# A hybrid attention and mixture-of-experts layer on Trainium2: the experts' slot table built by one-hot products, full-width attention products, 16 KB weight rows and a fifth early expert

## The chip, the cores and the metric

The kernel runs on one core of a Trainium2 chip. A core has TensorE (PE in the profile; PEld is its loading of weights), VectorE (DVE), ScalarE (ACT), GpSimd (POOL) and SyncE (SP), and 16 DMA engines that move data between DRAM, SBUF (the working memory of 128 partitions) and PSUM (where TensorE adds up its products). The metric is the device time of one execution in microseconds. It is compared between kernels as a median over several runs on the same chip.

## The reference

One layer works on 1024 tokens of width 1024. Cut to what matters here:

```python
h = rms_norm(x, ln1_g); proj = h @ w_in
attn = rms_norm(neighbourhood_attention(aq, ak, av, rpb), attn_out_g)   # 8 heads x 64
dn   = bidirectional_gated_deltanet(...)                                # 4 heads x 128, both directions
x = x + concat([attn, dn]) @ w_out
# hierarchical MoE on h = rms_norm(x, ln2_g):
gsel = argmax(h @ wg_r + bg_r)                  # 1 of 8 groups, its softmax probability gp
top_val, top_idx = top_k(expert logits of that group, 2)
gates = gp * softmax(top_val); eid = gsel * 8 + top_idx
# every expert e of 64, for its tokens:
hid = silu(xb @ w_gate[e]) * (xb @ w_up[e]);  y[token] += gate * (hid @ w_down[e])
x = x + y
```

In the attention each of the 16 rows of 64 tokens sees a window of 8 rows by 16 columns. A token goes to exactly two experts, and an expert gets as many tokens as chose it.

## The kernel before

**Up to the attention.** The projections and the DeltaNet scan take the first 545 us and are not touched.

**Attention and out-projection (about 545 to 785 us).** The list `blocks` holds 64 blocks of 128 queries of one head (`half`, head pair `pr`, column window `w`, head `h`). `attn_step(i)` issues the logits of block i, the transposes of block i-2 and the values of block i-3, so that three blocks are in flight. `attn_logits` (L605) makes 384 logits per query in f32r (a rounded format of f32) by two products that add up in `pq`: L617 is the high part of the keys with the high and low parts of the queries stacked over 128 partitions, L618 the low part `kl` of the keys, which has only the 64 rows of one head. VectorE adds the bias and takes the maximum (L621), ScalarE takes the exponential (L623), VectorE divides by the sum (L624, L625). `attn_turn` transposes the result in three squares on TensorE (L631), and ScalarE copies it to `pT` (L633). `attn_values` (L636) multiplies by the values: the two heads of a pair write to the two halves of the 128 output partitions, three products of 64 output partitions and 128 columns each (L641). One f32 product is two passes in the trace. VectorE copies the pair's result to `aT` (L644). Between the blocks the same loop issues the out-projection of the DeltaNet part (`dn_pre`, `dn_turn2`, `dn_mm2`, with `mm3` at L84 to L86: three f32r products of 128x512), and after half of the blocks the list `tail`.

**The tail (about 785 to 838 us).** `tail` runs five stages in a software pipeline over the eight tiles of 128 tokens: `ao_pre`, `ao_mm` (out-projection of the attention part), `router_turn`, `router_pick` (logits, group, two experts, gates: nearly all small VectorE instructions), and `router_rank`. The last finds each token's place among its expert's tokens by products with ones (L863, L864) and a masked sum on VectorE (L866), works out the slot number (L868), and two indirect DMAs per tile from POOL's queue scatter a 16-byte row (token, token, gate, norm factor) to the DRAM table `tbl` at expert * 1024 + rank (L870). The pools decide the final order; the ranks of all tiles and seven of the eight picks fall after 785 us.

**Weights.** `load_w` (L901) loads an expert by three DMAs of 1 MB: gate, up and down, 8 KB per partition and DMA. Four experts are loaded early, each released by a stage of the tail (the end of the attention, `ao_mm` of tiles 4, 6 and 7). There are 7 buffers for gate-and-up pairs and 6 for down (`room`).

**Experts (about 858 to 1437 us).** 32 steps take two experts each, 64 token slots per expert (`CAP`). The table for the slots is read back from DRAM as `tS` by four DMAs (L953, two on ACT's queue and two on SP's): `tS[0]` are ranks 0 to 63, `tS[1]` ranks 64 to 127 for the second pass of those steps that need one. VectorE fills the four gather buffers with zeros (L957). POOL gathers the rows of the tokens from DRAM (L962), TensorE transposes them (L970), multiplies with gate and up (L984) and down (L1002), and POOL adds the result to the output by an indirect DMA (L1005). Gathers run three steps ahead. After step 0's loads, a buffer's next load is issued on SP's queue and waits until the step that used the buffer is done with it.

Of the kernel before, what the change touches and what calls it, by code (L numbers as in the profile page):

```python
# [10 lines left out]
I32 = mybir.dt.int32  # L11
# [25 lines left out]
def tile_layer(ctx, tc, a, out):  # L37
# [545 lines left out]
    for w in range(4):  # L583
        for r in range(4):
            src = av_d.rearrange("(g r c) f -> r c g f", g=4, r=4)[r, KC0[w]:KC0[w] + 32]
            sp.dma_start(vw[r * 32:(r + 1) * 32, w], src)
    blocks = [(half, pr, w, h) for half in range(2) for pr in range(AH // 2) for w in range(4) for h in range(2)]
    qks, lgs, bts, pvs, pTs = {}, {}, {}, {}, {}

    def load_qk(half, pr):  # L590
# [3 lines left out]
        kl = a2.tile([64, 2, 768], F32R, name="kl")  # L594
# [32 lines left out]
    def attn_turn(i):  # L627
        lg = lgs.pop(i)
# [3 lines left out]
        pTs[i] = a2.tile([P, 3, P], F32, name="pT")  # L632
# [33 lines left out]
    atp = mix.enter_context(tc.tile_pool(name="atp", bufs=1, reuse_waits="tile"))  # L666
    aTs.append(atp.tile([P, AH // 2, S // 2], F32, name="aT"))
# [4 lines left out]
    wop = mix.enter_context(tc.tile_pool(name="wop", bufs=1, reuse_waits="tile"))  # L672
# [69 lines left out]
    iot = rc.tile([P, 64], F32, name="iot")  # L742
# [8 lines left out]
    def router_consts():  # L751
# [376 lines left out]
```

## Time and profile before

| | before |
|---|---|
| median of 3 runs | 1443.97 us (1441.38 to 1446.45) |
| profiled execution | 1439.0 us; span of the trace 1437.2 us |
| mean granted clock of TensorE | 0.951 |
| busy in the span: PE, DVE, ACT, POOL | 1254.6 us (87%), 645.8 us, 392.0 us, 374.8 us |
| moved by DMA | 346.97 MB, mean 241 GB/s |

The profiled execution is one run, 5.0 us below the median. Times of the rows below count from the start of its span. A granted clock of 1.00 is 2.4 GHz, 0.50 is 1.2 GHz. A matmul's row gives the time from its start to its modelled end, and matmuls overlap, so the price of one is the distance from its start to the next start. The 16 DMA engines together can show a share slightly above 1.

### The profile page before, as it was taken

How to read it: one execution, taken by the hardware profiler on the slowest of the kernel's cores; microseconds unless marked ns; L12 is line 12 of the kernel's file. 1: busy time of each engine (PE TensorE's matmuls, PEld its weight loads, DVE VectorE, ACT ScalarE, POOL GpSimd, SP SyncE). 2: the span in 40 equal slices, each digit the busy share in tenths (PEclk: the TensorE clock that was granted, in tenths of full speed). 3: DMA queues.
4: the chain of work that ended last, by engine and by line, in shares of the span. 5: the costliest groups of instructions: out<-in, count | busy, mean ns of one | idle time of the engine just before them, and what ended most of it. 6: DMA issues, size and time to landing. Idle time of an engine off the chain costs nothing. (4 is left out here: it accounts for less than half of the span.)

```text
span 1437.2 us, 20602 instructions
## 1 busy us (share of the span) xinstructions
PE 1254.6 (87%) x7425; PEld 840.1 (58%) x7426; DVE 645.8 (45%) x1541; ACT 392.0 (27%) x797; POOL 374.8 (26%) x427
## 2 busy tenths in 40 slices
PE   5988999969989996799999928998988888989985
PEld 4766889969978795477667823443333333423431
DVE  6456853853667643666755841222121121212211
ACT  4445422322354532775444310000000000000000
POOL 2046313021656543122110332112111111111200
PEclk9999999989999997899999959999999999999998
DMA  3261247355565469998673958999999999999981
GB/s 129 72 128 55 67 132 175 96 137 138 167 170 152 121 180 264 255 293 230 181 190 112 352 161 328 385 404 401 394 398 392 389 387 379 375 372 354 378 342 22
DMA packets 128553, 346.97 MB, mean 241 GB/s; under 512 B 53664, under 2 KB 59808, under 8 KB 103600
## 3 DMA queue, kind: packets, MB, share of 16 engines
q1 hardware_dynamic: 88048, 257.60, 50.3%
q0 software_dynamic: 27984, 71.94, 19.1%
q10 hardware_dynamic: 12400, 15.84, 3.2%
q8 instruction: 72, 1.18, 0.3%
q14 instruction: 49, 0.40, 0.1%
HBM read 305.39 MB, written 62.98 MB: 256 GB/s over the span
## 5 line engine op out<-in xcount | busy, mean ns | idle before, releaser
L984 PE MATMUL pp<-wg,xT 128*64 128x512 f32 x1216 | 300.5, 619 | 34.2 <-DMA wg<-in_w_up 25.1
L984 PEld LDWEIGHTS pp<-wg,xT 128*64 128x64 f32 x1216 | 119.5, 142 | 209.5 <-issue 202.2
L1005 POOL DMA_INDIRECT out<-yg,tS x38 | 60.3, 1587 | 409.0 <-DVEq L1050 265.0
L990 DVE SCALAR_TENSOR_TENSOR sg<-pp,tS,sg 128x256 f32<-128x256 f32 x38 | 18.4, 483 | 315.2 <-ACT sg L989 315.2
L1002 PE MATMUL po<-wd,hT 128*64 128x512 f32 x608 | 140.5, 605 | 20.4 <-ACTq L1050 12.6
L84 PE MATMUL pA<-w_hi,h_hi 128*128 128x256 f32 x512 | 151.2, 295 | 0.9 <-issue 0.9
L989 ACT ACTIVATE sg<-pp,tS 128x256 f32<-128x256 f32 x38 | 18.0, 473 | 486.6 <-PE pp L984 486.6
L85 PE MATMUL pA<-w_lo,h_hi 128*128 128x256 f32 x512 | 149.7, 292 | 0.0
L86 PE MATMUL pA<-w_hi,h_lo 128*128 128x256 f32 x512 | 149.7, 292 | 0.0
L1004 DVE TENSOR_SCALAR yg<-po,tS 128x512 f32<-128x512 f32 x76 | 57.1, 751 | 119.9 <-PE po L1002 119.9
L84 PEld LDWEIGHTS pA<-w_hi,h_hi 128*128 128x128 f32 x512 | 100.2, 196 | 2.2 <-issue 1.6
L85 PEld LDWEIGHTS pA<-w_lo,h_hi 128*128 128x128 f32 x512 | 100.2, 196 | 0.2
L86 PEld LDWEIGHTS pA<-w_hi,h_lo 128*128 128x128 f32 x512 | 100.0, 195 | 0.3
L1002 PEld LDWEIGHTS po<-wd,hT 128*64 128x64 f32 x608 | 40.7, 138 | 94.1 <-issue 66.4
L84 PE MATMUL pA<-h_hi,w_hi 128*128 128x512 f32 (+1 forms) x208 | 83.2, 400 | 1.3 <-ACT w_hi L75 1.3
L86 PE MATMUL pA<-h_hi,w_lo 128*128 128x512 f32 (+1 forms) x208 | 82.7, 398 | 0.0
L85 PE MATMUL pA<-h_lo,w_hi 128*128 128x512 f32 (+1 forms) x208 | 82.6, 397 | 0.0
L76 DVE TENSOR_TENSOR w_lo<-w_raw,w_hi 128x512 fp32r<-128x512 f32 (+1 forms) x60 | 40.3, 682 | 85.7 <-ACT w_hi L75 85.4
L970 PEld LDWEIGHTS pt<-ident,xg 128*128 128x128 f32 x304 | 37.4, 195 | 50.7 <-issue 30.0
L641 PE MATMUL pv<-pT,vw 128*64 128x128 f32 x384 | 57.7, 288 | 8.5 <-ACT pT L633 8.4
L239 DVE SCALAR_TENSOR_TENSOR acc<-raw,convw,acc 128x1024 f32<-128x1024 f32 x48 | 63.6, 1334 | 2.5 <-ACT acc L237 2.1
L970 PE MATMUL pt<-ident,xg 128*128 128x128 f32 x304 | 44.9, 291 | 20.5 <-DMA xg<-x_d,tS 20.5
(304 smaller groups left out, 2238.3 us busy)
## 6 DMA issues: line engine op xcount, KB each, us to landing
wd<-in_w_down SPq DMA_DIRECT2D x62, 1024.0 KB, 24.0
wg<-in_w_gate SPq DMA_DIRECT2D x61, 1024.0 KB, 23.7
wg<-in_w_up SPq DMA_DIRECT2D x61, 1024.0 KB, 23.5
bt<-in_bias SPq DMA_DIRECT2D x24, 384.0 KB, 5.4
w_raw<-in_w_nat SPq DMA_DIRECT2D x32, 256.0 KB, 3.6
w_raw<-in_w_dn SPq DMA_DIRECT2D x24, 256.0 KB, 3.1
k<-kk_d POOLq DMA_DIRECT2D x16, 384.0 KB, 8.9
SA_d<-cm POOLq DMA_DIRECT2D x8, 512.0 KB, 2.9
```

Source lines behind the costliest of these rows:

```text
L76: dve.tensor_sub(lo[:, k:k + 2], raw, hi[:, k:k + 2].bitcast(F32))
L84: pe.matmul(dst, sh, mh, start=(i == 0), stop=False)
L85: pe.matmul(dst, sh, ml, start=False, stop=False)
L86: pe.matmul(dst, sl, mh, start=False, stop=(i == n - 1))
L239: dve.scalar_tensor_tensor(acc, raw[:, t:t + S], convw[:, m, t:t + 1], acc, op0=OP.mult, op1=OP.add)
L641: pe.matmul(pv[h * 64:h * 64 + 64], vw[:, w, half + g, hc:hc + AD], pT[:, g], start=(g == 0), stop=(g == 2))
L970: pe.transpose(pt[:, k, :n], xg[:n, g * 4 + k:D:NK], ident[:n, :n])
L984: pe.matmul(pp[d * CAP:(d + 1) * CAP], xT[:, k, d * CAP:(d + 1) * CAP], ws[d][0][:, :, k * 256:(k + 1) * 256], start=(k == 0), stop=(k == ...
L990: dve.scalar_tensor_tensor(sg[:n], pp[:n, 1], mf[:n, 3:4], sg[:n], op0=OP.mult, op1=OP.mult)
L1002: pe.matmul(po[d * CAP:(d + 1) * CAP], hT[:, k, d * CAP:(d + 1) * CAP], w[1][:, k * D + c * 512:k * D + (c + 1) * 512], start=(k == 0), st ...
L1004: dve.tensor_scalar(yg[:n, cs], po[:n], mf[:n, 2:3], None, op0=OP.mult)
L1005: ins = pool.indirect_dma_start(out=out, out_offset=bass.IndirectOffsetOnAxis(ap=meta[:n, 0:1], axis=0), in_=yg[:n], in_offset=None, bound ...
```

## The change

- **Table.** For each tile `router_pick` now also makes `vals`: for each of the token's two choices its one-hot row over 64 experts times three numbers (token minus a large constant, gate, norm factor). `router_rank` makes `ro`, the one-hot row of the rank over 128 ranks, and two f32 products `ro`^T x `vals` (L893) add the tile's entries to the table in `pq`, which VectorE adds to `tab` (128 ranks x 64 experts x 3) in SBUF. After the last tile VectorE cuts `tS` out of `tab` (L972, L973). The scatters to `tbl` stay, since the rare case of an expert with more than 128 tokens reads it.
- **Order.** The gather buffers and `tS` are allocated in the tail, POOL instead of VectorE fills the buffers with zeros, and the last scatters are put behind the first gathers. The memory for this comes from the out-projection's weights and the second `aT`, whose pool is now closed in the tail (`opj`).
- **Fifth expert.** A fifth expert's load is issued right behind the fourth's. The buffers stay 7 and 6.
- **Weight rows.** The host stores gate and up side by side, so a gate-and-up pair is one DMA of 2 MB with 16 KB per partition.
- **Attention.** `kl` gets 64 more partitions that are zero, in two buffers that are cleared once, so that L618 (now L621) is a full 128x128 product. The values of a head pair are one product for both heads (128 output partitions, 256 columns, three per pair, now L646), of which the two diagonal blocks are copied out by two VectorE copies. One of the four `lg` buffers goes.

```diff
+    kls = [a1.tile([P, 2, 768], F32R, name=f"kl{i}") for i in range(2)]
+    for kl in kls:
+        pool.memset(kl[64:128].bitcast(F32), 0.0)
     blocks = [(half, pr, w, h) for half in range(2) for pr in range(AH // 2) for w in range(4) for h in range(2)]
-    qks, lgs, bts, pvs, pTs = {}, {}, {}, {}, {}
...
-        pool.dma_start(kl, heads(kk_d[pr // 2, :, 1, pr % 2, ks]))
+        pool.dma_start(kl[0:64], heads(kk_d[pr // 2, :, 1, pr % 2, ks]))
...
-        pe.matmul(pqv, q2[0:64, h, w * P:(w + 1) * P], kv(kl[:, h]), start=False, stop=True)
+        pe.matmul(pqv, q2[:, h, w * P:(w + 1) * P], kv(kl[:, h]), start=False, stop=True)
-        lg = lgs[i] = a2.tile([P, 384], F32, name="lg", bufs=4)
+        lg = lgs[i] = a2.tile([P, 384], F32, name="lg", bufs=3)
...
...
-        act.activation(pTs[i], pt[:, 0:3], AF.Copy)
+        if h == 0:
+            pTs[i // 2] = a2.tile([P, 3, 2, P], F32, name="pT")
+        act.activation(pTs[i // 2][:, :, h], pt[:, 0:3], AF.Copy)
     def attn_values(i):
         half, pr, w, h = blocks[i]
         if h == 0:
-            pvs[i // 2] = psQ.tile([P, P], F32, name="pv", bufs=1)
-        pv, pT, hc = pvs[i // 2], pTs.pop(i), (pr * 2 + h) * AD
+            return None
+        pv, pT = psQ.tile([P, 2, P], F32, name="pv", bufs=1), pTs.pop(i // 2)
         for g in range(3):
-            pe.matmul(pv[h * 64:h * 64 + 64], vw[:, w, half + g, hc:hc + AD], pT[:, g], start=(g == 0), stop=(g == 2))
-        if h == 1:
-            av = aTs[half][:, pr].rearrange("p (r c) -> p r c", c=64)[:, :, w * 16:w * 16 + 16]
-            return dve.tensor_copy(av, pv.rearrange("p (r c) -> p r c", c=16))
+            pe.matmul(pv, vw[:, w, half + g, pr * P:(pr + 1) * P], pT[:, g], start=(g == 0), stop=(g == 2))
+        av = aTs[half][:, pr].rearrange("p (r c) -> p r c", c=64)[:, :, w * 16:w * 16 + 16]
+        for h in range(2):
+            hs = slice(h * 64, h * 64 + 64)
+            ins = dve.tensor_copy(av[hs], pv[hs, h].rearrange("p (r c) -> p r c", c=16))
+        return ins
...
+        vt = o2.tile([P, 2, 3], F32, name="vt")
+        GATE = vt[:, :, 1]
+        dve.tensor_copy(vt[:, :, 0], tokm[:, t:t + 1].to_broadcast([P, 2]))
+        dve.tensor_copy(vt[:, :, 2], rt[:, 2:3].to_broadcast([P, 2]))
+        vals = o2.tile([P, 2, 64, 3], F32, name="vals", bufs=1)
+        for c in range(2):
+            dve.tensor_tensor(vals[:, c], o64[:, c, :, None].to_broadcast([P, 64, 3]),
+                              vt[:, c, None, :].to_broadcast([P, 64, 3]), op=OP.mult)
+        rts[t] = o64, EID, RNK, row, vals
     def router_rank(t):
-        o64, EID, RNK, row = rts.pop(t)
+        o64, EID, RNK, row, vals = rts.pop(t)
         pn = psQ.tile([P, P], F32, name="pv", bufs=1)
         for u in range(t):
             pe.matmul(pn[:, :64], onesb, oh[:, u], start=(u == 0), stop=False)
         pe.matmul(pn[:, :64], before, oh[:, t], start=(t == 0), stop=True)
         for c in range(2):
             dve.scalar_tensor_tensor(o64[:, c], o64[:, c], 1.0, pn[:, :64], op0=OP.mult, op1=OP.mult, accum_out=RNK[:, c:c + 1])
+        ro = o2.tile([P, 2, P], F32, name="ro", bufs=1)
+        pl = psQ.tile([P, 384], F32, name="pq")
+        for c in range(2):
+            dve.tensor_scalar(ro[:, c], iot, RNK[:, c:c + 1], None, op0=OP.is_equal)
+        for c in range(2):
+            pe.matmul(pl[:, :192], ro[:, c], vals[:, c].rearrange("p e v -> p (e v)"), start=(c == 0), stop=(c == 1))
+        pv3 = pl[:, :192].rearrange("p (e v) -> p e v", v=3)
+        if t == 0:
+            dve.tensor_copy(tab, pv3)
+        else:
+            dve.tensor_tensor(tab, tab, pv3, op=OP.add)
...
-            for j, n in enumerate(("w_down",) if i else ("w_gate", "w_up")):
-                ins = eng.dma_start(w if i else w[:, j], a[n][e].rearrange("(p k) f -> p (k f)", p=P))
-                if after is not None:
-                    tc.add_manual_dep(ins.ins, after.ins.name, mybir.DependencyInfo(how, mybir.DependencyReason.DATA),
-                                      reason="more urgent transfers first")
+            ins = eng.dma_start(w, a[("w_gu", "w_down")[i]][e])
+            if after is not None:
+                tc.add_manual_dep(ins.ins, after.ins.name, mybir.DependencyInfo(how, mybir.DependencyReason.DATA),
+                                  reason="more urgent transfers first")
...
+        if f is ao_mm and t == NT - 1:
+            opj.close()
+            mwB = ctx.enter_context(tc.tile_pool(name="mwB", bufs=1, side="right", reuse_waits="tile"))
+            m1 = ctx.enter_context(tc.tile_pool(name="m1", bufs=1, side="right", reuse_waits="tile"))
+            wt.setdefault(steps[2][1], [[], []])[0] += load_w(mwB, steps[2][1], after=ins)
+            tS = [m1.tile([P, 32, 4], I32, name=f"tS{i}") for i in range(2)]
+            ln2p = m1.tile([P, NK], F32, name="ln2p")
+            act.dma_start(ln2p, a["ln2"][:, 1])
+            LA = 3
+            xgb = [m1.tile([P, D], F32, name=f"xg{i}") for i in range(LA + 1)]
+            for x in xgb:
+                pool.memset(x, 0.0)
+    for tl in range(2):
+        for d in range(2):
+            src = tab[tl * CAP:(tl + 1) * CAP, d * 32:(d + 1) * 32]
+            dst = tS[tl][d * 64:(d + 1) * 64]
+            dve.tensor_scalar(dst[:, :, 0], src[:, :, 0], OOB, None, op0=OP.add)
+            dve.tensor_copy(dst[:, :, 2:4].bitcast(F32), src[:, :, 1:3])
...
-    mwG = ctx.enter_context(tc.tile_pool(name="mwG", bufs=3, reuse_waits="tile"))
-    mwD = ctx.enter_context(tc.tile_pool(name="mwD", bufs=2, reuse_waits="tile"))
+    mwG = ctx.enter_context(tc.tile_pool(name="mwG", bufs=2, reuse_waits="tile"))
+    mwD = ctx.enter_context(tc.tile_pool(name="mwD", bufs=1, reuse_waits="tile"))
     psX = ctx.enter_context(tc.tile_pool(name="psX", bufs=2, space=PSUM, reuse_waits="tile"))
-    ln2p = m1.tile([P, NK], F32, name="ln2p")
-    act.dma_start(ln2p, a["ln2"][:, 1])
-    tS = [m1.tile([P, 32, 4], I32, name=f"tS{i}") for i in range(2)]
-    tv = tbl.rearrange("(d e r) w -> d r e w", d=2, r=S)
-    for tl in range(2):
-        for d in range(2):
-            (act, sp)[d].dma_start(tS[tl][d * 64:(d + 1) * 64], tv[d, tl * CAP:(tl + 1) * CAP])
-    LA = 3
-    xgb = [m1.tile([P, D], F32, name=f"xg{i}") for i in range(LA + 1)]
-    for x in xgb:
-        dve.memset(x, 0.0)
...
+    for i in placed[-2:]:
+        tc.add_manual_dep(i.ins, ins.ins.name, mybir.DependencyInfo(mybir.DependencyClass.NoSync, mybir.DependencyReason.DATA),
+                          reason="the first rows are more urgent")
...
-            mw = mwA if n % room[part] < 4 else (mwG, mwD)[part]
+            mw = mwA if n % room[part] < 4 else mwB if n % room[part] == 4 else (mwG, mwD)[part]
```

The order in which the engines get the work changes at three places. The rows are the program's instructions in their order on one engine; x3 is three alike in a row. The first place is **TensorE in the middle of the attention**: `pt` are the transposes, `pv` the values, `pq` the logits, `pA` the out-projection. Before:

```order
L631 MATMUL pt<-ident,lg 128x128 x3
L641 MATMUL pv<-pT,vw 64x128 x3
L617 MATMUL pq<-k_6231,q_6230 128x384
L618 MATMUL pq<-kl,q_6230 128x384
L631 MATMUL pt<-ident,lg 128x128 x3
L641 MATMUL pv<-pT,vw 64x128 x3
```

After the change:

```order
L634 MATMUL pt<-ident,lg 128x128 x3
L646 MATMUL pv<-pT,vw 128x256 x3
L728 MATMUL pA<-ident,ot 128x128 x4
L620 MATMUL pq<-k_5640,q_5639 128x384
L621 MATMUL pq<-kl_5110,q_5639 128x384
L634 MATMUL pt<-ident,lg 128x128 x3
L620 MATMUL pq<-k_5640,q_5639 128x384
L621 MATMUL pq<-kl_5110,q_5639 128x384
```

The products of 64 output partitions and those of 64 contracted rows are gone; the values come once per pair instead of once per head. The second place is **VectorE at the end of the tail**, from the rank of the last tile on (`cnt` and `ci` are the counts per expert, which decide whether a second pass is run). Before:

```order
L866 SCALAR_TENSOR_TENSOR o_8247,gk<-o_8247,pv 128x64 x2
L868 SCALAR_TENSOR_TENSOR slot<-gk 128x2
L931 COPY cnt<-pv 1x64
L932 TENSOR_TENSOR ci<-cnt 1x32
L934 TENSOR_TENSOR x_8290<-cnt,lim 1x896
L935 TENSOR_REDUCE cnt<-x_8290 1x64
L936 CAST ci<-cnt 1x64
L937 TENSOR_REDUCE lim<-cnt 1x1
L938 CAST ci<-lim 1x1
L957 MEMSET xg_8338 128x1024
```

After the change:

```order
L886 SCALAR_TENSOR_TENSOR o_8255,gk<-o_8255,pv 128x64 x2
L891 TENSOR_SCALAR ro<-iot,gk 128x128 x2
L900 SCALAR_TENSOR_TENSOR slot<-gk 128x2
L898 TENSOR_TENSOR tab<-tab,pq 128x192
L982 COPY cnt<-pv 1x64
L972 TENSOR_SCALAR tS_8052<-tab 64x32
L973 COPY tS_8052<-tab 64x32x2
L972 TENSOR_SCALAR tS_8052<-tab 64x32
L973 COPY tS_8052<-tab 64x32x2
```

The one-hot rows, the addition to `tab` and the first two halves of `tS` now stand between the last rank and the counts' arithmetic, and the fills with zeros are gone from VectorE. The third place is **POOL's queue at the same point**. Before:

```order
L870 DMA tbl<-row,slot 65536x4 x4
L962 DMA xg_8338<-x_d,tS_8332 128x1024
L962 DMA xg_8339<-x_d,tS_8332 128x1024
L962 DMA xg_8340<-x_d,tS_8332 128x1024
L908 DMA wg<-in_w_gate 128x2048
```

After the change:

```order
L966 MEMSET xg_8059 128x1024
L902 DMA tbl<-row,slot 65536x4 x2
L51 TENSOR_TENSOR rt<-rt,mhalf 128x1
L902 DMA tbl<-row,slot 65536x4 x4
L1001 DMA xg_8056<-x_d,tS_8052 128x1024
L1001 DMA xg_8057<-x_d,tS_8052 128x1024
L1001 DMA xg_8058<-x_d,tS_8052 128x1024
L902 DMA tbl<-row,slot 65536x4 x2
```

The fills with zeros now stand ahead of the tail's last scatters, and the gathers ahead of the last tile's two scatters.

## Rows read from the trace of the kernel before

**Rows 1.** The profile's page: costliest groups, and a DMA issue with its median landing.

```profile
L984 PE MATMUL pp<-wg,xT 128*64 128x512 f32 x1216 | 300.5, 619 | 34.2 <-DMA wg<-in_w_up 25.1
...
xg<-x_d,tS POOLq DMA_INDIRECT x38, 11.0
```

**Rows 2.** Busy time by stretch: PE, PEld, DVE, ACT, POOL, clock, DMA share, GB/s.

```profile
594.00:785.00 191.00, 188.65 (x986) 132.60 (x985) 124.46 (x460) 108.61 (x236) 31.09 (x47) 1.00 0.76 206
785.00:824.00 39.00, 39.00 (x250) 33.88 (x248) 31.36 (x142) 14.96 (x33) 13.49 (x16) 1.00 0.95 346
824.00:838.00 14.00, 7.59 (x58) 6.89 (x58) 10.74 (x86) 3.48 (x12) 6.47 (x7) 0.71 1.00 350
838.00:859.00 21.00, 0.58 (x8) 0.40 (x7) 6.78 (x14) 1.28 (x1) 5.82 (x6) 0.50 0.30 30
...
882.00:888.00 6.00, 5.31 (x26) 1.57 (x22) 0.11 (x1) 0.47 (x1) 0.00 (x0) 1.00 0.41 77
888.00:1393.00 505.00, 446.46 (x1998) 188.96 (x2000) 110.08 (x173) 29.52 (x69) 90.28 (x68) 0.98 1.00 384
```

**Rows 3.** TensorE's timeline in the attention: start, duration, line, operation, tile.

```profile
649.07 0.44 PE L617 MATMUL pq<-k,q 128*128 128x384 f32 x1
649.45 0.44 PE L618 MATMUL pq<-kl,q 64*128 64x384 f32 x1
649.82 0.55 PE L631 MATMUL pt<-ident,lg 128*128 128x128 f32 x3
...
655.52 0.40 PE L86 MATMUL pA<-wo_hi,t_lo 128*128 128x512 f32 x1
655.76 0.39 PE L84 MATMUL pA<-wo_hi,t_hi 128*128 128x512 f32 x1
656.08 0.87 PE L641 MATMUL pv<-pT,vw 128*64 128x128 f32 x6
656.88 0.50 PE L85 MATMUL pA<-wo_lo,t_hi 128*128 128x512 f32 x1
657.22 0.39 PE L86 MATMUL pA<-wo_hi,t_lo 128*128 128x512 f32 x1
```

**Rows 4.** TensorE's timeline in the DeltaNet stage: full-width f32 passes of 256 columns.

```profile
441.25 1.13 PE L529 MATMUL ps<-w,kd 128*128 128x256 f32 x4
442.22 1.12 PE L544 MATMUL pw<-wc,at 128*128 128x128 f32 x8
```

**Rows 5.** TensorE's groups, 594 to 785 us: passes, then busy us and mean ns.

```profile
L641 PE MATMUL pv<-pT,vw 128*64 128x128 f32 x352 | 51.5, 283 | 0.1
```

**Rows 6.** VectorE's groups by form, 785 to 838 us.

```profile
L844 DVE TENSOR_SCALAR o<-iot,gk 128x64 f32<-128x64 f32 x14 | 3.0, 256 | 0.1
...
L834 DVE TENSOR_TENSOR ig<-rlg,rt 128x64 f32<-128x64 f32 x7 | 1.9, 271 | 0.1
...
L854 DVE COPY row<-gk 128x2 f32<-128x2 f32 x7 | 1.2, 164 | 0.1
```

**Rows 7.** VectorE's timeline, 836 to 848 us: the slot number behind the last rank.

```profile
838.09 0.16 DVE L868 SCALAR_TENSOR_TENSOR slot<-gk 128x2 int32<-128x2 f32 x1
```

**Rows 8.** POOL's timeline, 835 to 860 us; in brackets the idle time ahead.

```profile
854.73 1.06 POOL L962 DMA_INDIRECT xg<-x_d,tS  x1 [13.73 <-DMA tS<-tbl]
```

**Rows 9.** TensorE's timeline, 830 to 890 us.

```profile
859.15 1.97 PE L970 MATMUL pt<-ident,xg 128*128 128x128 f32 x8 [20.46 <-DMA xg<-x_d,tS]
...
880.22 7.09 PE L984 MATMUL pp<-wg,xT 128*64 128x512 f32 x32 [0.36 <-DVE xT L971]
```

**Rows 10.** SyncE's queue, 820 to 900 us: issues of DMAs.

```profile
823.64 0.33 SPq L908 DMA_DIRECT2D wg<-in_w_gate  x1
...
887.33 0.34 SPq L908 DMA_DIRECT2D wg<-in_w_gate  x1
```

**Rows 11.** DMA queues, 9 to 20 us: packets, MB, share of 16 engines.

```profile
q10 hardware_dynamic: 630, 1.09, 26.2%
q1 hardware_dynamic: 653, 0.51, 14.0%
```

More of the change, by code (lines that the diff above doesn't have):

```diff
@@ L586, in tile_layer @@
             sp.dma_start(vw[r * 32:(r + 1) * 32, w], src)
+    kls = [a1.tile([P, 2, 768], F32R, name=f"kl{i}") for i in range(2)]
+    for kl in kls:
+        pool.memset(kl[64:128].bitcast(F32), 0.0)
     blocks = [(half, pr, w, h) for half in range(2) for pr in range(AH // 2) for w in range(4) for h in range(2)]
-    qks, lgs, bts, pvs, pTs = {}, {}, {}, {}, {}
+    qks, lgs, bts, pTs = {}, {}, {}, {}
     def load_qk(half, pr):
@@ L593, in load_qk @@
         k2 = a2.tile([P, 2, 768], F32R, name="k2")
-        kl = a2.tile([64, 2, 768], F32R, name="kl")
+        kl = kls[pr % 2]
         heads = lambda v: v.rearrange("(h e) t -> e h t", h=2)
@@ L627, in attn_turn @@
     def attn_turn(i):
-        lg = lgs.pop(i)
+        lg, h = lgs.pop(i), blocks[i][3]
         pt = psQ.tile([P, 4, P], F32, name="pt")
@@ L631, in attn_turn @@
             pe.transpose(pt[:, g], lg[:, g * P:(g + 1) * P], ident)
-        pTs[i] = a2.tile([P, 3, P], F32, name="pT")
-        act.activation(pTs[i], pt[:, 0:3], AF.Copy)
+        if h == 0:
+            pTs[i // 2] = a2.tile([P, 3, 2, P], F32, name="pT")
+        act.activation(pTs[i // 2][:, :, h], pt[:, 0:3], AF.Copy)
     def attn_values(i):
@@ L665, in tile_layer @@
     prj.close()
-    atp = mix.enter_context(tc.tile_pool(name="atp", bufs=1, reuse_waits="tile"))
-    aTs.append(atp.tile([P, AH // 2, S // 2], F32, name="aT"))
     rc = mix.enter_context(tc.tile_pool(name="rc", bufs=1, reuse_waits="tile"))
     o2 = mix.enter_context(tc.tile_pool(name="o2", bufs=2, reuse_waits="tile"))
-    wop = mix.enter_context(tc.tile_pool(name="wop", bufs=1, reuse_waits="tile"))
+    opj = ExitStack()
+    atp = opj.enter_context(tc.tile_pool(name="atp", bufs=1, reuse_waits="tile"))
+    aTs.append(atp.tile([P, AH // 2, S // 2], F32, name="aT"))
+    wop = opj.enter_context(tc.tile_pool(name="wop", bufs=1, reuse_waits="tile"))
     dng = rc.tile([P, 1], F32, name="dng")
@@ L741, in tile_layer @@
     br = rc.tile([P, 72], F32, name="br")
-    iot = rc.tile([P, 64], F32, name="iot")
+    iot = rc.tile([P, P], F32, name="iot")
+    tokm = rc.tile([P, NT], F32, name="tokm")
+    tab = rc.tile([P, 64, 3], F32, name="tab")
     tokc = rc.tile([P, NT], F32, name="tokc")
@@ L760, in router_consts @@
         sp.dma_start(br, a["b_r"].to_broadcast([P, 72]))
-        pool.iota(iot, pattern=[[1, 64]], base=0, channel_multiplier=0, allow_small_or_imprecise_dtypes=True)
+        pool.iota(iot, pattern=[[1, P]], base=0, channel_multiplier=0, allow_small_or_imprecise_dtypes=True)
         pool.iota(tokc, pattern=[[P, NT]], base=0, channel_multiplier=1, allow_small_or_imprecise_dtypes=True)
+        dve.tensor_scalar(tokm, tokc, -OOB, None, op0=OP.add)
         pool.memset(onesb, 1.0)
@@ L838, in router_pick @@
         dve.tensor_copy(mf[:, 1], mi[:, 1])
-        gk = o2.tile([P, 3, 2], F32, name="gk")
-        GATE, EID, RNK = (gk[:, i] for i in range(3))
+        gk = o2.tile([P, 2, 2], F32, name="gk")
+        EID, RNK = (gk[:, i] for i in range(2))
+        vt = o2.tile([P, 2, 3], F32, name="vt")
+        GATE = vt[:, :, 1]
         dve.scalar_tensor_tensor(EID, gs.to_broadcast([P, 2]), 8.0, mf[:, 1, 0:2], op0=OP.mult, op1=OP.add)
@@ L843, in router_pick @@
         for c in range(2):
-            dve.tensor_scalar(o64[:, c], iot, EID[:, c:c + 1], None, op0=OP.is_equal)
+            dve.tensor_scalar(o64[:, c], iot[:, 0:64], EID[:, c:c + 1], None, op0=OP.is_equal)
         dve.tensor_tensor(oh[:, t], o64[:, 0], o64[:, 1], op=OP.add)
@@ L1019, in tile_layer @@
     loads = [(2 * j + d, part) for j in range(2, NS) for part in range(2) for d in range(2)]
+    loads = [l for l in loads if l[0] != 4]
     first = next(i for i, (n, part) in enumerate(loads) if n == room[part])
@@ L1092, in layout @@
     a["b_r"] = np.concatenate([g["router_group_b"][0], g["router_expert_b"][0]])[None]
-    a["w_gate"], a["w_up"], a["w_down"] = (g[f"expert_w_{n}"][0] for n in ("gate", "up", "down"))
+    gate, up, down = (g[f"expert_w_{n}"][0].reshape(64, P, 2048) for n in ("gate", "up", "down"))
+    a["w_gu"], a["w_down"] = np.stack([gate, up], 2), down
     a["w_out"] = g["w_out"][0].reshape(NK, P, D).transpose(1, 0, 2)
```

2 lines of the change are left out of this document (removed).

## The prediction, made before the changed kernel was run

> **What bounds the kernel now.** I went from the end to the start. In the expert stage one product, L984, has 300.5 us of TensorE's time and most of its waits there are for the weights' DMAs [rows 1]. From 888 to 1393 us the DMA engines have a share of 1.00 at 384 GB/s while TensorE is busy 446 of 505 us [rows 2]: the stage is bound by the weights that are still to come (64 pairs of gate and up less the 7 that fit, 64 downs less 6: 180 MB), and it moves as a whole when its start moves. The start is bad: from 838 to 859 us TensorE works 0.58 of 21 us and the DMAs carry 30 GB/s [rows 2]. This gap is the way through the table in DRAM. Ahead of it, 594 to 785 us, TensorE is busy 188.65 of 191 us with VectorE at 124 and ScalarE at 109: what comes off TensorE there comes off the time until VectorE or ScalarE is full. In the tail, 785 to 824, TensorE is busy all 39 us, but VectorE 31.36 of them, and from 824 to 838 VectorE has 10.74 of 14 us and TensorE 7.59. So TensorE bounds the first half of the change, VectorE is second in the tail, a chain of single steps bounds the table, and DMA the rest.
>
> **Attention.** The two logit products of a block start 0.38 us apart and the next operation 0.37 later: 0.75 us a block. An out-projection product of 512 columns and full width starts 0.24 after its like (655.52 to 655.76) [rows 3], so 384 columns are worth 0.18 and the pair 0.36. Between a saving of nothing (384 columns cost what they cost) and 0.39 I take 0.30, near the upper end, since the out-projection's passes are of the same f32r kind. The values of one head take 0.80 (656.08 to 656.88); the interval ahead of them is 0.32 and the one behind 0.34 where alike neighbours have 0.24, so 0.18 more, and a pair costs 1.96. Six full-width f32 passes of 256 columns cost 0.24 each (four in 0.97 us) [rows 4], 1.45 in all. That is 0.5 per pair; where a value product stands next to L618 the two share such a step, so I take 0.4. The stretch has 352 passes [rows 5], six per block: 58 blocks or 29 pairs, and 55 blocks of logits, as these run three ahead. 55 x 0.30 + 29 x 0.4 = 28 us less for TensorE; the bounds are 4 (0.15 a pair, nothing for logits) and 36.
>
> The longer intervals stand only beside products that use 64 columns or 64 rows. The Trainium skill, "TensorEngine Tiling (Array Packing)", section Key Properties, says that a change of the tiling mode drains TensorE. The trace agrees, with 0.08 to 0.10 us beside L641; if narrow products had no such price, the values would give only 4 of the 12 us and the sum would be 8 us higher.
>
> VectorE has one more copy per pair, 29 x 0.27 (a 128x64 form) [rows 6] = 8 us. It then has 132 of 163 us, 82%, ScalarE 67%. With three blocks in flight, one step late shows, so I count four fifths of 28: **-22** (bounds 0 and -30). The first load of `kl` comes behind two clears; that is under 2 us of POOL's time ahead of the stretch and inside the bounds.
>
> **Tail.** VectorE's additions per tile, by their nearest rows: two small copies at 0.16; two products to `vals`, 128x192, between 0.27 (one of 64 columns) and three times that, taken at 0.37, since most of a 64-column instruction is a fixed part (128x2 costs 0.16); two `ro` at 0.26; one addition to `tab` at 0.37 [rows 6]. That is 1.06 in a pick and 0.89 in a rank. Seven picks and eight ranks lie between 785 and 838: 14.5 us on 42.1 of 53. It does not fit (56.6): at least 3.6 us are exposed, at most 14.5. Since VectorE's instructions there wait for each other and for TensorE, I take 10, half of it before 824: **+5**, the other half in the next part. The four fills by POOL cost VectorE nothing, as POOL has 13.5 of 39 us.
>
> **Table.** Before: the instruction behind the last rank's masked sums starts at 838.09 [rows 7]. POOL issues the first gather at 854.73, after 13.73 us of waiting for `tS` [rows 8], and TensorE transposes at 859.15 [rows 9]: 21.1 us, of which the gather itself is 4.4. After: two `ro` 0.52; four passes of 192 columns, 0.18 each at full clock and 0.36 at the granted 0.50 of this stretch, 1.3; `tab` 0.37; the counts' copy 0.2; the four instructions of `tS[0]` 0.8; the gather 4.4; handovers between engines 0.4. That is 8.0, so 13 us less, with 5 of the tail against it: **-8**. The fifth expert lies across it: the fourth's load is issued at 823.64 [rows 10] and keeps the DMAs busy to 838; 3.1 MB more at 384 GB/s end near 846. If the tail is 5 us longer, the gather is issued there and finds the queues free; if it isn't, the gather lands like those of the expert stage, 11.0 instead of 4.4 [rows 1]. Either way about 851. I keep -3 to -13. Scatters behind the gathers wait for nobody.
>
> **Fifth expert by itself: 0.** Between 882 and 888 the DMAs carry 77 GB/s [rows 2] although most weights are still to come: all 7 and 6 buffers are full. SP's next load is issued at 887.33 [rows 10], when the second pass of step 0 is done with its gate-and-up product (880.22 + 7.09) [rows 9]. The number of buffers is the same after, so loading the fifth sooner only fills them sooner. What moves the bound stage is that step 0 starts, and so frees buffers, 8 us earlier. That is in the sum.
>
> **16 KB rows.** Two queues in a quiet stretch of 11 us (176 us of engine time) spend 26.2% on 630 packets and 1.09 MB and 14.0% on 653 packets and 0.51 MB [rows 11]. Both fit 8.5 ns per packet and 37.4 us per MB, an estimate from these two rows. Half the packets of the 57 gate-and-up pairs behind the gap saved, 57 x 128 x 8.5 ns / 16 = 3.9 us: **-4** (0, if the hardware cuts them up again, to -5). TensorE's 34.2 us of waits for weights [rows 1] can take that up.
>
> **Sum:** -22 + 5 - 8 - 4 = -29 on the profiled execution's 1439.0 us (its span is 1437.2): 1410. The median of the runs shown is 5.0 above that execution, so the forecast is **1415 us**.
>
> **Rivals.** (a) *The attention gives little* (0.17): the 0.37 us are what 384 columns cost, or VectorE's 82% in a chain PE, VectorE, ScalarE, VectorE, PE holds TensorE up. For it: ScalarE and VectorE have waits of their own in each block. Against: TensorE waited for nearly nothing in 191 us. With -4 there, -11 in all: 1433. (b) *All of it comes* (0.12): -30, tail 0, -10, -4 make -44: 1400. (c) *The fifth expert gives its 8 us as well* (0.08), if the buffers fill later than I think: 1407. Against it stands the idle DMA at 882. (d) *Slower* (0.08): VectorE becomes the bound of attention and tail. All 14.5 us of the tail and the 8 us of copies are exposed and TensorE's saving turns into waits: +22.5 - 13 - 4 = +5.5, 1449. It decides from the point where VectorE's work of a block exceeds TensorE's; by the rows it has 132 against 163 us, so it would need 30 us more than I count. That the change does not do what it says shows in (a).
>
> **How the numbers follow.** The forecast has 0.55. The range 1399 to 1435 takes in (a), (c) and about half of (b), and leaves out (d) and the rest; the likeliest case alone has 1406 to 1424. Within 0.3% (4.3 us, about what a measurement of this kernel can tell from no change) are part of (a) and part of (d), 0.07; slower is most of (d), 0.05; faster the rest, 0.88.
>
> **What would show it.** Right: value products of 256 columns starting about 0.24 us apart; the logit pair in 0.36 to 0.45; no added interval beside them; the stretch from 594 to 785 some 22 us shorter with TensorE still near 100%. In the tail VectorE above 90% and `ao_mm` of tile 7 about 17 us earlier rather than 22. First transposes about 8 us after the last masked sum. The DMAs idle again before the first buffer comes free, as at 882. A GB/s one per cent higher from then on. Wrong: TensorE with waits for `lg` or `pT` in the attention; a gather that takes 10 us; or a first free buffer that does not come earlier though step 0 starts earlier.

## The result, and the profile after

The changed kernel takes 1426.86 us (median of 4 runs, 1423.81 to 1431.12) against 1442.85 us for the kernel before on the same chip: ratio 0.9888, 95% interval 0.9855 to 0.992. That is 16 us less (12 to 21), where 29 were forecast. The profiled span is 1424.4 us against 1437.2; the profiled execution of the kernel before (1439.0 us) lies 4 us below this median and that of the changed kernel (1426.66) at its median, so differences between the two traces run 3 to 4 us short of the 16. Where the two traces stand at the same points of the program (us from the start of the span; "later" is after minus before):

| point of the program | before | after | later |
|---|---|---|---|
| VectorE takes the logits of block 8 | 593.61 | 586.15 | -7.5 |
| the same of block 63, the last | 778.16 | 774.39 | -3.8 |
| last out-projection of the attention part ends on VectorE | 823.61 | 823.25 | -0.4 |
| last masked sum of the ranks ends | 838.05 | 840.22 | +2.2 |
| first transposes of gathered rows | 859.15 | 848.44 | -10.7 |
| first load behind a freed buffer | 887.33 | 875.61 | -11.7 |
| end of the span | 1437.2 | 1424.4 | -12.8 |

So the table gave what it was to give, and of the attention, the largest term of the sum, hardly anything is left at the last out-projection. The stretches of the changed kernel, with the columns of [rows 2] (PE, PEld, DVE, ACT, POOL, clock, DMA share, GB/s):

```profile
586.20:823.30 237.10, 207.14 (x1065) 168.35 (x1065) 174.07 (x669) 123.34 (x268) 48.55 (x67) 0.95 0.80 230
823.00:840.00 17.00, 11.32 (x69) 10.29 (x70) 13.73 (x106) 3.81 (x12) 6.69 (x8) 0.65 0.95 342
840.00:848.00 8.00, 2.25 (x12) 1.52 (x11) 4.91 (x23) 1.28 (x1) 3.09 (x4) 0.50 0.65 249
868.00:875.00 7.00, 6.59 (x33) 2.21 (x32) 1.04 (x2) 0.00 (x0) 1.66 (x1) 1.00 0.32 49
876.00:1382.00 506.00, 444.51 (x2002) 167.02 (x2004) 110.16 (x173) 29.70 (x70) 90.31 (x68) 0.98 0.98 385
```

The first row is the stretch from block 8's logits to the last out-projection; below it is called **the stretch**. TensorE is idle for 30 of its 237 us. Before it had next to no idle time there [rows 2], as the same stretch of that kernel shows:

```profile
593.60:823.60 230.00, 227.65 (x1234) 166.68 (x1233) 155.82 (x603) 123.96 (x269) 44.59 (x63) 1.00 0.79 230
```

TensorE does get its saving, 20.5 us of busy time, and the stretch is not shorter for it. In these two traces it is 7 us longer, 3.7 of them up to block 63 and 3.4 in the tail. Two experiments below leave the code of the stretch as it is in the changed kernel (e7) and in the kernel before (e8); their rows:

```profile
591.30:825.00 233.70, 204.27 (x1065) 166.39 (x1065) 174.23 (x669) 123.40 (x268) 48.56 (x67) 0.96 0.82 234
598.00:831.90 233.90, 232.26 (x1233) 170.04 (x1233) 155.99 (x603) 124.13 (x269) 44.82 (x63) 0.97 0.77 226
```

So single traces of the same code differ by 3 to 4 us here. That the stretch is no shorter is shown, that it is longer is not. What TensorE waits for in the changed kernel's stretch, longest first (total, times, longest):

```profile
PE pq L620 <- DVE mx L624: 9.9, 6, 4.2
PE pA L84 <- ACT t_hi L731: 5.7, 1, 5.7
PE pA L84 <- ACT wo_hi L693: 3.8, 2, 2.6
PE pt L634 <- DVE mx L627: 3.5, 2, 2.2
PE pt L634 <- DVE lg L628: 3.4, 3, 1.9
```

These are waits for VectorE and ScalarE, and these two wait for loads: 39 us together in the changed kernel's stretch, where it is 9 in that of the kernel before. The two longest of the changed kernel, then the longest of the kernel before:

```profile
ACT wo_hi L693 <- DMA wo_raw<-in_w_out: 16.6, 5, 5.9
DVE lg L624 <- DMA bt<-in_bias: 9.5, 4, 3.0
```

```profile
ACT wo_hi L685 <- DMA wo_raw<-in_w_out: 6.4, 3, 4.3
```

One wait of TensorE over all engines, 634.9 to 639 us:

```profile
636.22 0.76 DVE L770 TENSOR_TENSOR wr<-wr,ln 128x576 f32<-128x576 f32 x1 [4.33 <-DMA wr<-in_w_r]
637.57 0.55 DVE L624 CUSTOM_DVE_ANT_0 lg<-pq,bt 128x384 f32<-128x384 f32 x1
...
638.18 0.69 PE L620 MATMUL pq<-k,q 128*128 128x384 f32 x1 [4.22 <-DVE mx L624]
```

VectorE's instructions stand here in the program's order. One of them (L770, which scales the router's weights) stands for 4.33 us behind a load; the maximum of a block (L624) is queued behind it; TensorE stands for 4.22 us because that maximum must free `pq`. The products themselves came out as read. TensorE's timeline:

```profile
639.68 0.79 PE L84 MATMUL pA<-wo_hi,t_hi 128*128 128x512 f32 x1 [0.49 <-DVE ms L719]
640.27 0.63 PE L85 MATMUL pA<-wo_lo,t_hi 128*128 128x512 f32 x1
...
648.76 0.39 PE L86 MATMUL pA<-wo_hi,t_lo 128*128 128x512 f32 x1
648.99 0.34 PE L620 MATMUL pq<-k,q 128*128 128x384 f32 x1
649.17 0.34 PE L621 MATMUL pq<-kl,q 128*128 128x384 f32 x1
649.35 0.49 PE L634 MATMUL pt<-ident,lg 128*128 128x128 f32 x3
...
650.42 1.56 PE L646 MATMUL pv<-pT,vw 128*128 128x256 f32 x6
651.82 0.60 PE L728 MATMUL pA<-ident,ot 128*128 128x128 f32 x4
...
848.44 1.97 PE L1009 MATMUL pt<-ident,xg 128*128 128x128 f32 x8 [5.91 <-DMA xg<-x_d,tS]
```

The logit pair takes 0.36 us (648.99 to 649.35) where it took 0.75 [rows 3], the six passes of a value pair 1.40 (650.42 to 651.82) where two heads took 1.96, and no longer interval stands beside them.

### The profile page after: what moved, and what is told of

The parts are those of the page before. It is cut to its first block, busy times and chain, and to the rows that moved or that the text cites. A ratio compares the mean times of both kernels' runs of the same rounds, so it can differ in the third digit from the quotient of the medians.

```text
span 1424.4 us, 20268 instructions
## 1 busy us (share of the span) xinstructions
PE 1230.5 (86%) x7265; PEld 820.3 (58%) x7266; DVE 663.0 (47%) x1634; ACT 391.3 (27%) x797; POOL 379.2 (27%) x428
## 5 line engine op out<-in xcount | busy, mean ns | idle before, releaser
L1023 PE MATMUL pp<-wg,xT 128*64 128x512 f32 x1216 | 296.8, 613 | 37.3 <-DMA wg<-in_w_gu 24.1
L1023 PEld LDWEIGHTS pp<-wg,xT 128*64 128x64 f32 x1216 | 96.1, 141 | 232.2 <-issue 189.8
L84 PE MATMUL pA<-w_hi,h_hi 128*128 128x256 f32 x512 | 150.5, 294 | 0.7 <-issue 0.7
L85 PE MATMUL pA<-w_lo,h_hi 128*128 128x256 f32 x512 | 149.1, 291 | 0.0
L86 PE MATMUL pA<-w_hi,h_lo 128*128 128x256 f32 x512 | 149.0, 291 | 0.0
L84 PEld LDWEIGHTS pA<-w_hi,h_hi 128*128 128x128 f32 x512 | 99.7, 195 | 1.6 <-issue 1.1
L85 PEld LDWEIGHTS pA<-w_lo,h_hi 128*128 128x128 f32 x512 | 99.8, 195 | 0.2
L86 PEld LDWEIGHTS pA<-w_hi,h_lo 128*128 128x128 f32 x512 | 99.4, 194 | 0.3
L84 PE MATMUL pA<-h_hi,w_hi 128*128 128x512 f32 (+1 forms) x208 | 83.6, 402 | 1.8 <-ACT w_hi L75 1.8
L85 PE MATMUL pA<-h_lo,w_hi 128*128 128x512 f32 (+1 forms) x208 | 83.2, 400 | 0.0
L86 PE MATMUL pA<-h_hi,w_lo 128*128 128x512 f32 (+1 forms) x208 | 82.8, 399 | 0.0
L84 PE MATMUL pA<-wo_hi,t_hi 128*128 128x512 f32 x128 | 54.4, 425 | 10.0 <-ACT t_hi L731 5.7
L75 ACT ACTIVATE w_hi<-w_raw 128x512 fp32r<-128x512 f32 (+1 forms) x60 | 35.5, 611 | 76.2 <-DMA w_raw<-in_w_nat 37.6
## 6 DMA issues: line engine op xcount, KB each, us to landing
k<-kk_d POOLq DMA_DIRECT2D x16, 384.0 KB, 10.7
```

Source lines behind the costliest of these rows:

```text
L75: act.activation(hi[:, k:k + 2], raw, AF.Copy)
L84: pe.matmul(dst, sh, mh, start=(i == 0), stop=False)
L85: pe.matmul(dst, sh, ml, start=False, stop=False)
L86: pe.matmul(dst, sl, mh, start=False, stop=(i == n - 1))
L1023: pe.matmul(pp[d * CAP:(d + 1) * CAP], xT[:, k, d * CAP:(d + 1) * CAP], ws[d][0][:, :, k * 256:(k + 1) * 256], start=(k == 0), stop=(k == ...
```

## The experiments

The theories, as the expectations name them. **A**: TensorE's saving is real, but VectorE and ScalarE stand behind loads, and TensorE had covered that. **B**: three `lg` buffers instead of four hold TensorE. **C**: the added VectorE copies and VectorE's own work do.

**e1: the attention part alone, on the kernel before.** All attention lines of the diff ahead of the prediction, among them:

```diff
-        pe.matmul(pqv, q2[0:64, h, w * P:(w + 1) * P], kv(kl[:, h]), start=False, stop=True)
+        pe.matmul(pqv, q2[:, h, w * P:(w + 1) * P], kv(kl[:, h]), start=False, stop=True)
-        lg = lgs[i] = a2.tile([P, 384], F32, name="lg", bufs=4)
+        lg = lgs[i] = a2.tile([P, 384], F32, name="lg", bufs=3)
```

> The kernel before with the attention part alone (full-width logits and values, three lg buffers). Theory A (the saving on TensorE is real, but VectorE and ScalarE stand still behind loads, and TensorE had covered that): TensorE's busy time falls by 22 to 26 us, its waits between 545 and 785 us rise by about as much, and the time falls by 0 to 6 us, 1437 to 1443. The recorded forecast: 22 us less, 1421.

Measured: 1431.15 us (10 runs) against 1442.35, ratio 0.993, interval 0.9911 to 0.995: 10 us less. Neither number was hit: the forecast gave 22 less, theory A at most 6. From 545 to 785 us TensorE is busy for 20.5 us less (196.53 instead of 217.08), where theory A had 22 to 26, and idle for as much longer. In the trace the last out-projection ends at 817.71, 5.9 us sooner, all of it gained ahead of block 8 (587.27 instead of 593.61); the stretch is as long as before, with TensorE idle for 27.6 us of it:

```profile
587.30:817.70 230.40, 202.83 (x1047) 164.82 (x1048) 166.69 (x633) 123.61 (x268) 44.98 (x63) 0.96 0.82 233
```

The other 4 us of the shorter span lie behind the last out-projection, where executions differ by as much anyway (see e4). Why the first eight blocks went faster was not tested.

**e2: the changed kernel without the attention part.**

```diff
-        kl = kls[pr % 2]
+        kl = a2.tile([64, 2, 768], F32R, name="kl")
...
-            pe.matmul(pv, vw[:, w, half + g, pr * P:(pr + 1) * P], pT[:, g], start=(g == 0), stop=(g == 2))
+            pe.matmul(pv[h * 64:h * 64 + 64], vw[:, w, half + g, hc:hc + AD], pT[:, g], start=(g == 0), stop=(g == 2))
```

> The changed kernel with the attention part undone. If attention is worth 4 us at most (theories A, B and C alike): 1427 to 1432, and the last out-projection of the attention ends within 4 us of the changed kernel's. If it was worth what was forecast and the longer tail ate it: 1445 or more.

Measured: 1434.39 us, ratio 0.9952, interval 0.9929 to 0.9975: the table, the fifth expert and the rows together give 7 us. With e1's 10 that is 17, and the whole change measured 16: the two halves add up within their intervals. The expectation was 2 us too low. Its second half was missed by more: the last out-projection was to end within 4 us of the changed kernel's, and it ends at 834.89, 11.6 us later. Without any of the attention part the stretch is longer than before (230.0), in e1 (230.4) and in the changed kernel (237.1):

```profile
595.10:834.90 239.80, 235.48 (x1246) 172.69 (x1244) 162.75 (x638) 122.70 (x267) 48.76 (x67) 0.97 0.76 223
```

The longer tail is 3.7 us of it; most of the rest is TensorE's busy time at the lower clock. So inside the changed kernel the attention part is worth more at this point than on the kernel before (6 us in e1), by single traces.

**e3: four `lg` buffers in the changed kernel.**

```diff
-        ev = npool.tile([P, 2, 256], F32, name="ev")
+        ev = npool.tile([P, 2, 256], F32, name="ev", bufs=1)
...
-        lg = lgs[i] = a2.tile([P, 384], F32, name="lg", bufs=3)
+        lg = lgs[i] = a2.tile([P, 384], F32, name="lg", bufs=4)
```

> The changed kernel with four lg buffers instead of three (room made by one buffer less for the projections' results). Theory B (the third buffer holds TensorE): 10 us less or more, about 1416, and TensorE's waits for lg and for the maxima are halved. Theory A: within 3 us of the changed kernel, 1424 to 1430.

Measured: 1436.61 us, ratio 0.9961 to the kernel before, 10 us slower than the changed kernel. The run isn't clean, since `ev` lost a buffer for it: block 8's logits come at 597.37, 11 us late, 6 of which are there at block 0 (570.45 instead of 564.40), where `lg` can't matter yet. From there to the last out-projection it takes 238.5 us where the changed kernel takes 237.1. So theory B finds no support, though the run can't bound a smaller effect.

**e4: one bias tile.**

```diff
-            bts[half, pr, w] = a2.tile([P, 2, 384], F32, name="bt")
-            sp.dma_start(bts[half, pr, w], a["bias"][pr, w - w // 2, half])
+            if i == 0:
+                bts[0] = a2.tile([P, 2, 384], F32, name="bt", bufs=1)
+                sp.dma_start(bts[0], a["bias"][pr, w - w // 2, half])
+            bts[half, pr, w] = bts[0]
```

> The changed kernel with one bias tile loaded once and used for all blocks: the other 23 loads of 384 KB are left out, so that all but the first blocks get a wrong bias. Theory A: TensorE's waits between 560 and 785 us, some 35, fall below 18, and the time falls by 10 us or more, to 1416 or less. Theory B and theory C (the added VectorE copies): at most 4 us less, 1423 or more.

Measured: 1413.63 us, ratio 0.9794, interval 0.9751 to 0.9837. The time met theory A, the mechanism did not: the stretch is only 3 us shorter, as long as in e7 with all its bias loads, and TensorE is idle for 27 us of it.

```profile
584.40:818.30 233.90, 207.09 (x1079) 169.85 (x1078) 175.62 (x676) 124.24 (x270) 49.86 (x69) 0.95 0.72 201
```

Up to the last out-projection 5 us are won; 6 more appear after the first freed buffer (542.4 us to the end instead of 548.8), in a stage that the edit reaches only through the wrong routing (39 passes instead of 38). This part differs by some us between profiled executions anyway (549.9 before, 547.2 in e1, 545.8 in e2), so a total alone tells little here, and the next runs were read by the stretch.

**e5 and e6: neither bias nor output weights loaded, in the changed kernel (e5) and in the kernel before (e6).** e4's edit and:

```diff
-                raw = wop.tile([P, 512], F32, name="wo_raw", bufs=2)
-                sp.dma_start(raw, a["w_out"][:, half * 4 + k, n:n + 512])
+                if "wo" not in bts:
+                    bts["wo"] = wop.tile([P, 512], F32, name="wo_raw")
+                    sp.dma_start(bts["wo"], a["w_out"][:, half * 4 + k, n:n + 512])
+                raw = bts["wo"]
```

> The changed kernel with one bias tile and one raw tile of the out-projection's weights, each loaded once and used throughout: 23 bias loads of 384 KB and 15 weight loads of 256 KB are left out, so that bias and output weights are wrong; every engine's work stays. Theory A (loads hold VectorE and ScalarE, and these TensorE): from the logits of block 8 to the end of the last attention out-projection, 237 us in the changed kernel and 234 with one bias tile, 220 or less; time 1403 or less. Theory C (VectorE's own work and the chain between the engines): 230 or more, time 1408 or more.

> The kernel before with the same loads left out. Theory A says that TensorE covered them there: the same stretch, 230 us in the kernel before, stays at 224 to 230, and what is saved is at the attention's start only: time 1425 to 1440. If loads bound this kernel as well, the stretch falls by as much as in the changed kernel, to 215 or less.

The false weights change the routing, so that the expert stage has more passes (1945 and 1983 us in all); only the stretch counts. First e5, then e6:

```profile
586.60:796.50 209.90, 201.89 (x1083) 167.45 (x1081) 173.84 (x675) 123.80 (x269) 49.48 (x68) 0.99 0.72 198
```

```profile
583.20:816.50 233.30, 231.67 (x1243) 170.48 (x1244) 158.04 (x611) 125.76 (x273) 46.30 (x64) 0.98 0.63 174
```

This decides it. Without these loads the changed kernel's stretch falls by 27 us (24 from e7's), to 209.9 with 8 us of idle time on TensorE. The kernel before gains nothing from the same edit (233.3, where it has 230.0 and 233.9 with the loads): TensorE is busy for all but 1.6 us of it. With the loads the change doesn't shorten the stretch, without them it shortens it by 23, although the tail in it got longer. From block 8 to block 63 alone 161.1 us are left of 187.9: 27 of the 28 us that the prediction had for TensorE. The VectorE work is the same in e5 and in the changed kernel (174 us), so theory C falls. And e5 has three `lg` buffers, so theory B can hold no more than some of the 8 us that are left.

**e12: only the output weights not loaded**, in the changed kernel (e5 without e4's edit).

> The changed kernel with one raw tile of the output weights, loaded once (15 loads of 256 KB left out, so that the output weights are wrong and with them the routing: only the time up to the router counts); the bias is loaded as ever. If the conversion of the weights is what holds VectorE and ScalarE: from block 8's logits to the last attention out-projection 218 us or less, most of the 27 us that leaving out both brought. If it is the sum of the loads: 224 to 232, and TensorE's waits go on behind the bias and the DeltaNet outputs.

```profile
586.70:807.50 220.80, 205.93 (x1083) 170.71 (x1081) 174.09 (x675) 123.85 (x269) 49.58 (x68) 0.97 0.82 229
```

This is one execution. The stretch is 16 us shorter, between the two expectations (218 or less, 224 to 232). The bias alone was worth 3, no more than traces of the same code differ by, and both together 27: the weights hold most, and the rest shows once they are gone.

**e9 and e10: six raw buffers instead of two**, in the changed kernel (e9) and in the kernel before (e10).

```diff
     prj.close()
+    rwp = e4.enter_context(tc.tile_pool(name="rwp", bufs=6, side="right", reuse_waits="tile"))
...
-                raw = wop.tile([P, 512], F32, name="wo_raw", bufs=2)
+                raw = rwp.tile([P, 512], F32, name="wo_raw")
```

> The changed kernel with six instead of two buffers for the raw output weights (in a pool that lives only as long as the attention). Theory A, in its form after the runs with loads left out (the conversion of the output weights, two loads at a time, holds VectorE and ScalarE): from block 8's logits to the last attention out-projection 228 us or less instead of 237, ScalarE's waits for raw weights (16.6 us) below 8, time 1420 or less. The rival (what is short is the DMA engines' bandwidth in that stretch, not the number of buffers): at most 3 us less, 1423 or more, and the waits move to other loads.

> The kernel before with six buffers for the raw output weights. Theory A: TensorE is busy throughout and covers the conversion, so the same stretch stays within 3 us of 230 us and the time within 5 us of the kernel before, 1438 to 1445. If the buffers cost time there too: 8 us less or more, 1435 or less.

Measured: e9 1428.3 us, ratio 0.9897 (0.9868 to 0.9926), no gain on the changed kernel; e10 1455.75 us, ratio 1.0081 (1.0051 to 1.0111), 12 us slower than before, which neither theory had expected. e9 in two stretches, 560 to 600 us and the stretch:

```profile
560.00:600.00 40.00, 18.78 (x77) 13.77 (x76) 22.00 (x77) 21.97 (x42) 9.17 (x16) 0.65 0.92 235
600.00:828.60 228.60, 209.15 (x1077) 170.80 (x1075) 172.60 (x666) 119.45 (x262) 48.40 (x67) 0.96 0.81 229
```

The stretch does fall to 228.6, by 8.5 us (5 from e7's), and ScalarE's waits for raw weights from 16.6 to 6.5 us. The time is the rival's and the waits are theory A's, so these runs don't tell whether buffers or bandwidth is short. But block 8 comes at 600.04, 14 us later: the first eight blocks take 30.0 us instead of 21.7. In e10 they take 34.3 instead of 27.9, and its stretch is longer too, 241.1, where theory A had 227 to 233. The attention begins while the DMA engines are already full (share 1.03 from 560 to 600 in the changed kernel), and more weights loaded ahead there delay what the blocks need first. That the start got longer is measured; that the order of these loads is the reason is argued, and why e10's stretch got longer is open.

**e11: six raw buffers, and the table in DRAM cleared during the DeltaNet stage.** e9's edit and:

```diff
...
+    pad = dnp.tile([P, 32, 4], I32, name="pad")
+    pool.memset(pad[:, :, 1:4], 0.0)
+    pool.memset(pad[:, :, 0:1], int(OOB))
+    for b in range(64 * S // (32 * P)):
+        sp.dma_start(tblv[b], pad)
     dec.close()
...
-        for b in range(64 * S // (32 * P)):
-            sp.dma_start(tblv[b], pad)
```

> The changed kernel with six raw buffers, and the 16 transfers that clear the table in DRAM (1 MB in rows of 512 bytes) issued during the DeltaNet stage instead of in the middle of the attention. If the burst of loads around 600 to 630 us holds VectorE: 3 to 6 us less than with six buffers alone. If not: within 3 us of it.

Measured: 1428.35 us, ratio 0.9904 (0.9874 to 0.9933), the same as e9. Moving the clearing transfers out of the attention brings nothing that could be measured. Its stretch:

```profile
598.90:833.20 234.30, 210.50 (x1076) 171.91 (x1075) 172.20 (x666) 119.11 (x262) 48.27 (x67) 0.95 0.77 218
```

With the same six buffers this is as long as e7's with two, so the shorter stretch of e9 is not confirmed.

**e7: the fifth expert not early.**

```diff
-            wt.setdefault(steps[2][1], [[], []])[0] += load_w(mwB, steps[2][1], after=ins)
...
-    loads = [l for l in loads if l[0] != 4]
```

> The changed kernel with the fifth expert's load no longer behind the fourth's, but with the other loads of step 0, behind the first gathers. The recorded forecast (the buffers are full before the first comes free either way): 1424 to 1430, the first load behind a freed buffer at most 2 us later, and the DMAs still idle before it. The rival (the early load is worth its 3.1 MB): 6 to 8 us more, 1432 to 1436.

Measured: 1424.98 us, ratio 0.9882 (0.9843 to 0.9922), the same as the changed kernel's 0.9888. The first load behind a freed buffer comes at 876.35 instead of 875.61. One detail was wrong: the DMAs are not idle ahead of it, they are still at the load that came later. SyncE's first issue there and the stretch ahead of it:

```profile
876.35 0.34 SPq L939 DMA_DIRECT2D wg<-in_w_gu  x1
```

```profile
868.00:876.00 8.00, 7.58 (x40) 2.84 (x38) 1.78 (x3) 0.00 (x0) 1.65 (x1) 1.00 1.00 395
```

In the changed kernel the same place has a share of 0.32 (868 to 875, above). The early load moves work into a gap and leaves another gap behind.

**e8: 16 KB rows alone, on the kernel before.**

```diff
-            for j, n in enumerate(("w_down",) if i else ("w_gate", "w_up")):
-                ins = eng.dma_start(w if i else w[:, j], a[n][e].rearrange("(p k) f -> p (k f)", p=P))
...
+            ins = eng.dma_start(w, a[("w_gu", "w_down")[i]][e])
...
```

> The kernel before with gate and up side by side, one load of 16 KB rows per pair. The recorded forecast: 4 us less (0 to 5), 1437 to 1443, and half the packets of the weights' queue for gate and up. If the hardware cuts rows at 8 KB: the same packets and the same time.

Measured: 1440.18 us against 1443.27, ratio 0.9973, interval 0.9944 to 1.0003: the forecast's 4 us, but not told apart from nothing. The packets do fall, from 128,553 to 119,336; 64 x 128 = 8,192 of that are the halved gate-and-up rows; the page's row of e8:

```profile
DMA packets 119336, 346.96 MB, mean 240 GB/s; under 512 B 52640, under 2 KB 58784, under 8 KB 102576
```

No run was faster than the changed kernel beyond its interval and still computed the whole layer.

## Why the prediction was right in direction and too large

**The step that failed** is in the part on the attention: "With three blocks in flight, one step late shows, so I count four fifths of 28". TensorE's saving was read rightly. Its price rows came true (0.36 for the pair, 1.40 for the values), and without the loads its busy time in the stretch falls from 231.67 to 201.89 us, 30 against the 28 of the sum. But of the 22 that were counted next to none is seen in the stretch (e1: 230.4, against 230.0 us before and 233.9 in e8). The 10 us by which e1 is faster lie elsewhere: 6 ahead of block 8, for which the sum has no term, and the rest behind the stretch. That the total came as near to the forecast as it did is in part luck. I took VectorE's 82% and ScalarE's 67% as room. An average of busy time says nothing of an engine that stands in order behind a load. In the kernel before, the two stood 9 us behind loads in the stretch and TensorE was idle for 2; with a faster TensorE they stand for 39 and TensorE is idle for 30. The DMA share of 0.76 in [rows 2] was in front of me and I did not ask what the loads would do to a faster TensorE. The sign of being wrong that the prediction names, TensorE with waits for `lg` or `pT`, came true (3.4 and 1.6 us). Rival (a) (4 us there, 1433 in all) came nearer than the forecast, and had half the cause: VectorE does hold TensorE up, but behind loads, not by its own work.

**The clock took a part.** The changed kernel's stretch has a granted clock of 0.95 where the kernel before has 1.00 and e5 0.99, and the same products take 207.14 us busy in it and 201.89 in e5. So some 5 us of the loss are the clock. The two longest of the three pieces at 0.50:

```profile
586.20:599.40 13.20, 6.90 (x16) 5.18 (x17) 8.01 (x27) 8.60 (x14) 1.02 (x1) 0.50 1.09 302
637.00:643.80 6.80, 5.13 (x14) 3.83 (x14) 5.23 (x21) 2.86 (x7) 1.61 (x2) 0.50 0.60 230
```

The first came over from the attention's start. The second begins in the 4.22 us wait shown above, and the third (725.7 to 729.1) just behind a wait of 2.6 us. In the second L84 and L85 start 0.59 us apart where like products took 0.24 [rows 3]. A lower mean does not need long waits in the stretch: e8 has 0.97 with 1.7 us of idle time in it.

**The joins.** With one width throughout, L86 to L620 is 0.23 us again (648.76 to 648.99), without the 0.08 to 0.10 that stood beside the narrow products. The Trainium skill, "TensorEngine Tiling (Array Packing)", Key Properties, says that a change of the tiling mode drains TensorE; the trace agrees.

**Tail: +5 and +5 forecast, +6 measured.** From block 63's logits to the last out-projection 48.9 us instead of 45.5, and from there to the last masked sum 17.0 instead of 14.4. VectorE is at 13.73 of 17 us (second row of the stretches), 81%, where the prediction's sign was above 90%. The prices were right: `vals` 0.35 (0.37 forecast), `ro` 0.28 (0.26), `tab` 0.35 (0.37).

**Table: 8.0 us forecast, 8.2 measured** (840.22 to 848.44). The one-hot products took 1.65 us at a clock of 0.50, 0.35 more than counted; 0.14 of that is a slip in the sum, since four times 0.36 is 1.44 and not 1.3. POOL's first gather was issued at 843.99, and its rows were there 4.4 us later:

```profile
843.99 1.06 POOL L1001 DMA_INDIRECT xg<-x_d,tS  x1 [5.53 <-issue]
```

With the tail's 2.5 us against it this part gives -10 where -8 was forecast. The step 0 that starts 10.7 us sooner frees its first buffer 11.7 us sooner (875.61), and the bound stage moves as a whole, as the prediction said.

**Fifth expert: 0 forecast, 0 measured** (e7). Rival (c) falls. **Rows: -4 forecast, -3 (8 less to nothing) measured** (e8). In the changed kernel the GB/s of the bound stage, which were to be one per cent higher, are 385 where they were 384 [rows 2].

Rival (d), slower, would have needed VectorE as the bound; it has 174 of 237 us. The terms as measured, -10 for the attention, -12.9 + 6 for table and tail, 0 and -3, make -20; the measured -16 has an interval of -12 to -21.

What stays open: why the first eight blocks went faster, and whether an order of the loads exists that gives the whole 22. In e9 the shorter stretch was paid for at the attention's start, and e11 did not repeat it; a version that spreads the loads over the DeltaNet stage was not tried beyond the clearing of the table.

## What to carry to other kernels

An engine that is 100% busy hides what the others would wait for. Before counting a saving on it, list the loads that stand ahead of in-order instructions of the engines that feed it, since these waits can become its own. The test is cheap: leave the loads out in both kernels, and compare the same stretch. A chain of single steps through DRAM, in a gap where nothing else runs, was the safer gain here: its price added up instruction by instruction and moved the whole bound stage behind it.

## What was not expected of the hardware

A TensorE that waits can lose more than the wait: the granted clock fell to 0.50 in a wait of 4 us and stayed there for 6.8 us, in which products were 2.5 times as far apart (0.59 against 0.24 us). Waits and clock don't go in step, though: the mean was 0.95 with 30 us of idle time in 237 (part of the low clock came over from the attention's start) and 0.97 with 1.7 us in e8. And more loads in flight can cost: four more buffers of 256 KB for the output weights made the kernel before 12 us slower (e10).
